# Adaptive max pooling over windows of 16: three stores to memory become two

## The chip, the cores and the metric

The kernel runs on one core of a Trainium2 chip. The metric is the device time of one execution in microseconds, the median of several runs. Three engines matter here: VectorE (DVE in the profile) reduces, SyncE (SP) issues the loads and most stores, ScalarE (ACT) issues one store. The transfers themselves are carried out by the core's 16 DMA engines, whoever issues them.

## The reference

The input is 32 x 256 x 4096 numbers of 4 bytes (134.2 MB), the output 32 x 256 x 256 (8.4 MB). Since 4096 divides evenly by 256, every output is the maximum over 16 neighbours.

```python
batch, channels, length = 32, 256, 4096
output_size = 256
...
for i in range(output_size):
    start = int(i * length / output_size)
    end = int((i + 1) * length / output_size)
    result[:, :, i] = np.max(x[:, :, start:end], axis=-1)
```

## The kernel before

**Columns.** Rows and windows of the input are seen as one long list of windows of W = 16 numbers, 2,097,152 of them. Dealt out over the 128 partitions of the on-chip memory they make `total` = 16384 windows a partition, each of which gives one output column. The list is cut into two groups, of 9340 and 7044 columns a partition, one after the other in memory (`group`, line 64). Within a group each partition owns one unbroken stretch of input and of output, so a load or store is 128 long rows, one for each partition, with the group's length as the distance between rows.

**Loads.** `group_a` is one load of 128 columns, eight of 1024, and one of 1020; `group_b` is six of 1024 and one of 900 (`last`). A load of 1024 columns is 128 rows of 65,536 B, 8 MB. All loads are issued by SP in one queue (lines 87 and 96). The first group is taken from its end towards its beginning, the second from its beginning on.

**The ring.** Loads land in `ring`, two slots of 1024 columns with a GAP of 152 columns for each. Every second time a slot is used, the load is placed 152 columns further (`moved`). A load's reduction is split in two, of 872 and 152 columns (lines 98 to 101), the part that the next load into the slot overwrites going first, so that the next load may be issued when the larger part is done. The gaps leave room in the ring.

**Reductions.** VectorE does all of them, `pooled` on line 56: 32 instructions. Results go to the tile `kept` (15484 columns), but those of the last load, for which there is no room in `kept`, go into a free stretch of the ring (`last_kept`, lines 103 to 105).

**Stores.** Three. ScalarE stores the last 900 columns from the ring (line 114), rows of 3,600 B; it waits for the last reduction. After a scheduling barrier without waits (line 115), SP stores `kept` in two transfers (line 117), one for each group: 9340 columns (rows of 37,360 B), for which it waits for nothing that SP has not waited for already, and 6144 columns (rows of 24,576 B), for which it waits for the last reduction but one. SP's instructions run in the order of the program: 17 loads, then these two stores. Each load waits for the reduction that frees its place.

Of the kernel before, what the change touches and what calls it, by code (L numbers as in the profile page):

```python
# [1 line left out]

# [4 lines left out]


@with_exitstack
def kernel(  # L10
    ctx: ExitStack,
    tc: tile.TileContext,
    x: bass.AP,
    output_size: bass.AP,
    out: bass.AP,
):

    nc = tc.nc
    P = nc.NUM_PARTITIONS
    fp32 = mybir.dt.float32

    B, C, L = x.shape
    O = int(output_size)  # L30
    assert L % O == 0, (L, O)
    W = L // O
    total = B * C * O // P
    assert B * C * O % P == 0

    CHUNK = 1024
    GAP = 152
    FIRST = 128
    LOADS_A, LOADS_B = 9, 6

    LESS = 4
    group_a = [FIRST] + [CHUNK] * (LOADS_A - 1) + [CHUNK - LESS]
    last = total - sum(group_a) - LOADS_B * CHUNK
    group_b = [CHUNK] * LOADS_B + [last]
    assert 0 < last and last * (W + 1) <= CHUNK * W

    pool = ctx.enter_context(tc.tile_pool(name="pool", bufs=1))
    ring = pool.tile([P, 2 * (CHUNK + GAP) * W], fp32, tag="ring", name="ring")
    kept = pool.tile([P, total - last], fp32, tag="kept", name="kept")

    xw = x.flatten_outer_dims().rearrange("r (o w) -> (r o) w", w=W)
    ow = out.flatten_outer_dims().rearrange("r o -> (r o)")

    def pooled(dst, at, n):

        nc.vector.reduce_max(  # L56
            out=dst,
            in_=ring[:, at * W : (at + n) * W].rearrange("p (n w) -> p n w", w=W),
            axis=mybir.AxisListType.X,
        )  # L60

    taken = 0

    def group(n):

        nonlocal taken
        span = slice(taken * P, (taken + n) * P)
        taken += n
        return (
            xw[span].rearrange("(p n) w -> p (n w)", p=P),  # L70
            ow[span].rearrange("(p n) -> p n", p=P),
        )

    stores = []
    n_loads = 0
    base = 0
    for g, loads in enumerate((group_a, group_b)):
        xg, og = group(sum(loads))
        a = sum(loads) if g == 0 else 0
        for n in loads:  # L80
            if g == 0:
                a -= n
            xn = xg[:, a * W : (a + n) * W]
            dst = kept[:, base + a : base + a + n] if n != last else None
            if n == FIRST:

                nc.sync.dma_start(  # L87
                    out=ring[:, CHUNK * W : (CHUNK + n) * W], in_=xn
                )
                pooled(dst, CHUNK, n)  # L90
            else:

                low = n_loads % 2 * (CHUNK + GAP)
                moved = n_loads // 2 % 2
                at = low + moved * GAP
                nc.sync.dma_start(out=ring[:, at * W : (at + n) * W], in_=xn)
                if n != last:
                    cut = CHUNK - GAP if moved else GAP
                    parts = [(0, cut), (cut, n)]
                    for u, v in parts if moved else parts[::-1]:  # L100
                        pooled(dst[:, u:v], at + u, v - u)
                else:
                    end = (at + CHUNK) * W
                    last_kept = ring[:, end - n : end]
                    pooled(last_kept, at, n)
                n_loads += 1
            if g:
                a += n
        full = a - last if g else sum(loads)
        stores.append((og[:, 0:full], kept[:, base : base + full]))  # L110
        base += full
    assert taken == total

    nc.scalar.dma_start(out=og[:, full : full + last], in_=last_kept)
    tc.no_sync_barrier()
    for dst, src in stores:
        nc.sync.dma_start(out=dst, in_=src)


# [1 line left out]
_INS = ['x', 'output_size']  # L121
_OUTS = [((32, 256, 256), 'float32')]

_NUMBERS = {'output_size': 256}


# [26 lines left out]
```

## Time and profile before

| | us |
|---|---|
| median of 3 runs | 334.95 (334.94 to 335.01) |
| span of the profiled execution | 333.08 |
| VectorE busy | 276.5 |
| distance between two loads' landings | 19.35 |
| the two reductions of one load (872 + 152 columns) | 17.28 |
| VectorE's wait for each load | 2.07 |

The profile is of one execution; its span leaves out what lies around the program, here 1.87 us. A DMA issue on SP or ScalarE takes about 0.4 us of that engine; the transfer then goes on by itself, and "us to landing" is counted from the issue to the arrival of the last of 16 completion marks, one from each DMA engine. The trace also holds a record of every packet of every transfer, with start, duration, size and queue; here one packet is one row of one partition.

### The profile page before, as it was taken

To read this page: it belongs to the slowest core of one execution; us is meant where nothing else is said; L and a number is where in the kernel's file an instruction comes from. 1 tells how busy PE (TensorE), PEld (TensorE's weight loads), DVE (VectorE), ACT (ScalarE), POOL (GpSimd) and SP (SyncE) were. 2 spreads that over 40 slices of the span, in tenths; PEclk is the share of its full clock that TensorE was granted. 3 is DMA by queue.
4 is the path that set the end of the run, shared out by engine and by line. 5 is a ranking of instruction groups with operands and counts; after the bars stand their busy time and mean duration, and the time that the engine had idled before them with its cause. 6 is when DMAs were issued, how large, how long until landed. Compare 5 with 4: busy or idle time off the path is not lost.

```text
span 333.1 us, 113 instructions
## 1 busy us (share of the span) xinstructions
DVE 276.5 (83%) x32; POOL 0.2 (0%) x4
## 2 busy tenths in 40 slices
DVE  2009979797997979799797979979797998979993
POOL 0000000000000000000000000000000000000000
DMA  9898989899898989899898989899898989899997
GB/s 378 378 504 378 504 378 504 378 449 433 378 504 378 504 378 504 378 441 441 384 494 377 504 378 504 378 456 425 386 496 378 504 378 504 378 458 443 393 395 330
DMA packets 2880, 142.61 MB, mean 428 GB/s; under 512 B 320, under 2 KB 320, under 8 KB 448
## 3 DMA queue, kind: packets, MB, share of 16 engines
q1 hardware_dynamic: 2736, 142.15, 98.8%
q10 hardware_dynamic: 144, 0.46, 0.3%
HBM read 134.22 MB, written 8.39 MB: 428 GB/s over the span
## 4 chain that ended last, share of the span: by engine, by line
DMA 57%; DVE 36%; DVEq 5%; issue 0%; SPq 0%
DMA ring<-in_x_dram 57%; DVE kept L56 36%; DVEq L148 5%; SPq L87 0%
## 5 line engine op out<-in xcount | busy, mean ns | idle before, releaser
L56 DVE TENSOR_REDUCE kept<-ring 128x152 f32<-128x2432 f32 (+3 forms) x31 | 261.4, 8473 | 51.5 <-DMA ring<-in_x_dram 51.5
L56 DVE TENSOR_REDUCE ring<-ring 128x900 f32<-128x14400 f32 x1 | 15.1, 15143 | 0.0
L134 POOL MEMSET const-bfloat16-1.0<- 128x1 bf16 x1 | 0.1, 103 | 0.0
L134 POOL MEMSET const-uint8-127<- 128x1 uint8 x1 | 0.1, 102 | 0.0
L134 POOL MEMSET const-float32-0.0<- 128x1 f32 x1 | 0.1, 100 | 0.2 <-issue 0.2
L134 POOL MEMSET const-float32-1.0<- 128x1 f32 x1 | 0.1, 99 | 0.0
## 6 DMA issues: line engine op xcount, KB each, us to landing
ring<-in_x_dram SPq DMA_DIRECT2D x1, 8160.0 KB, 23.9
ring<-in_x_dram SPq DMA_DIRECT2D x1, 7200.0 KB, 21.7
out_dram<-kept SPq DMA_DIRECT2D x1, 4670.0 KB, 32.4
out_dram<-kept SPq DMA_DIRECT2D x1, 3072.0 KB, 18.2
ring<-in_x_dram SPq DMA_DIRECT2D x1, 1024.0 KB, 4.7
out_dram<-ring ACTq DMA_DIRECT2D x1, 450.0 KB, 4.2
ring<-in_x_dram SPq DMA_DIRECT2D x14, 24.0
```

What stands on the lines that cost most here:

```text
L56: nc.vector.reduce_max(out=dst, in_=ring[:, at * W : (at + n) * W].rearrange("p (n w) -> p n w", w=W), axis=mybir.AxisListType.X,)
L134: nc = _bacc.Bacc("TRN2", target_bir_lowering=False, num_devices=1)
L148: with _tile.TileContext(nc) as tc:
```

## The change

The two groups are cut elsewhere. The first now takes all loads but the last two: 128 columns, thirteen loads of 1024, one of 1020, which makes 14460 columns; the second takes the last two, of 1024 and 900 columns, 1924 in all. `kept` holds the first group alone. The second group's results all go to the last 1924 x 4 B of the ring (`tail_kept`). ScalarE stores these 1924 columns in one transfer (rows of 7,696 B), and SP the first group in one transfer (rows of 57,840 B). In the program ScalarE's store stands ahead of the barrier, as before. The engines' own order of instructions stays: SP has 17 loads and then one store, which waits for the 29th of VectorE's 32 reductions (the second one of the 1020-column load); VectorE has the same 32 reductions, the shorter of 868 columns now for the fifteenth load, not the tenth; the wait for the free stretch of the ring moves from the last reduction to the last but two.

```diff
-    LOADS_A, LOADS_B = 9, 6
-    LESS = 4
-    group_a = [FIRST] + [CHUNK] * (LOADS_A - 1) + [CHUNK - LESS]
-    last = total - sum(group_a) - LOADS_B * CHUNK
-    group_b = [CHUNK] * LOADS_B + [last]
+    LAST = 900
+    n_head = (total - FIRST - CHUNK - LAST) // CHUNK
+    short = total - FIRST - CHUNK - LAST - n_head * CHUNK
+    head = [FIRST] + [CHUNK] * n_head + [short]
+    tail = [CHUNK, LAST]
+    n_a, n_b = sum(head), sum(tail)
...
-    kept = pool.tile([P, total - last], fp32, tag="kept", name="kept")
+    kept = pool.tile([P, n_a], fp32, tag="kept", name="kept")
...
+    xa = xw[: n_a * P].rearrange("(p n) w -> p (n w)", p=P)
+    oa = ow[: n_a * P].rearrange("(p n) -> p n", p=P)
+    xb = xw[n_a * P :].rearrange("(p n) w -> p (n w)", p=P)
+    ob = ow[n_a * P :].rearrange("(p n) -> p n", p=P)
...
+    work = []
+    a = n_a
+    for n in head:
+        a -= n
+        work.append((n, xa[:, a * W : (a + n) * W], kept[:, a : a + n]))
+    tail_kept = ring[:, size - n_b :]
+    a = 0
+    for n in tail:
+        work.append((n, xb[:, a * W : (a + n) * W], tail_kept[:, a : a + n]))
+        a += n
...
+    for i, (n, xn, dst) in enumerate(work[1:]):
+        moved = i // 2 % 2
+        at = i % 2 * (CHUNK + GAP) + moved * GAP
+        load(at, n, xn)
+        if i == len(work) - 2:
+            pooled(dst, at, n)
+            continue
+        cut = CHUNK - GAP if moved else GAP
+        parts = [(0, cut), (cut, n)]
+        for u, v in parts if moved else parts[::-1]:
+            pooled(dst[:, u:v], at + u, v - u)
...
-    nc.scalar.dma_start(out=og[:, full : full + last], in_=last_kept)
+    nc.scalar.dma_start(out=ob, in_=tail_kept)
     tc.no_sync_barrier()
-    for dst, src in stores:
-        nc.sync.dma_start(out=dst, in_=src)
+    nc.sync.dma_start(out=oa, in_=kept[:, :])
```

More of the change, by code (lines that the diff above doesn't have):

```diff
@@ L38 @@
     FIRST = 128
-    LOADS_A, LOADS_B = 9, 6
-    LESS = 4
-    group_a = [FIRST] + [CHUNK] * (LOADS_A - 1) + [CHUNK - LESS]
-    last = total - sum(group_a) - LOADS_B * CHUNK
-    group_b = [CHUNK] * LOADS_B + [last]
-    assert 0 < last and last * (W + 1) <= CHUNK * W
-    pool = ctx.enter_context(tc.tile_pool(name="pool", bufs=1))
-    ring = pool.tile([P, 2 * (CHUNK + GAP) * W], fp32, tag="ring", name="ring")
-    kept = pool.tile([P, total - last], fp32, tag="kept", name="kept")
+    LAST = 900
+    n_head = (total - FIRST - CHUNK - LAST) // CHUNK
+    short = total - FIRST - CHUNK - LAST - n_head * CHUNK
+    assert 0 < short <= CHUNK
+    head = [FIRST] + [CHUNK] * n_head + [short]
+    tail = [CHUNK, LAST]
+    n_a, n_b = sum(head), sum(tail)
+    assert n_a + n_b == total
     xw = x.flatten_outer_dims().rearrange("r (o w) -> (r o) w", w=W)
     ow = out.flatten_outer_dims().rearrange("r o -> (r o)")
+    xa = xw[: n_a * P].rearrange("(p n) w -> p (n w)", p=P)
+    oa = ow[: n_a * P].rearrange("(p n) -> p n", p=P)
+    xb = xw[n_a * P :].rearrange("(p n) w -> p (n w)", p=P)
+    ob = ow[n_a * P :].rearrange("(p n) -> p n", p=P)
+    pool = ctx.enter_context(tc.tile_pool(name="pool", bufs=1))
+    size = 2 * (CHUNK + GAP) * W
+    ring = pool.tile([P, size], fp32, tag="ring", name="ring")
+    kept = pool.tile([P, n_a], fp32, tag="kept", name="kept")
     def pooled(dst, at, n):
@@ L60, in pooled @@
         )
[L62 to L111, printed above, removed]
@@ L112, with load @@
-    assert taken == total
-    nc.scalar.dma_start(out=og[:, full : full + last], in_=last_kept)
+    def load(at, n, xn):
+        nc.sync.dma_start(out=ring[:, at * W : (at + n) * W], in_=xn)
+    work = []
[8 more added lines that the diff above has]
+        a += n
+    n, xn, dst = work[0]
@@ new lines @@
+    load(CHUNK, n, xn)
+    pooled(dst, CHUNK, n)
+    for i, (n, xn, dst) in enumerate(work[1:]):
[3 more added lines that the diff above has]
+        if i == len(work) - 2:
+            assert (at + n) * W + n_b <= size
+            pooled(dst, at, n)
[4 more added lines that the diff above has]
+            pooled(dst[:, u:v], at + u, v - u)
```

## The prediction

> **What bounds the kernel now.** I read the page first, then the order in time, the transfers with their landings, and transfers alone in short windows near the end.
>
> ```profile
> span 333.1 us, 113 instructions
> ...
> DVE 276.5 (83%) x32; POOL 0.2 (0%) x4
> ...
> q1 hardware_dynamic: 2736, 142.15, 98.8%
> q10 hardware_dynamic: 144, 0.46, 0.3%
> ```
>
> q1 is the queue that SP issues to, q10 ScalarE's. Together their packets keep the 16 DMA engines busy for 99.1% of the span; VectorE is busy for 83%. Bytes through the DMA engines are the bound, and an edit that moves the same bytes can only win what lies at the two ends. What matters here is the end, in the order of time:
>
> ```profile
> 291.37 21.90 SPq L117 DMA_DIRECT2D out_dram<-kept  x2
> 295.62 17.28 DVE L56 TENSOR_REDUCE kept<-ring 128x872 f32<-128x13952 f32 x2 [2.07 <-DMA ring<-in_x_dram]
> 312.82 15.14 DVE L56 TENSOR_REDUCE ring<-ring 128x900 f32<-128x14400 f32 x1
> 327.99 0.37 ACTq L114 DMA_DIRECT2D out_dram<-ring  x1
> ```
>
> The last reduction has no idle time before it: from the landing of the last load but one (295.60 in the chain of waits) VectorE runs without a break to 327.97, and ScalarE's store goes out at 327.99. The transfers show what the DMA engines do meanwhile:
>
> ```profile
> ring<-in_x_dram SPq DMA_DIRECT2D x1, 7200.0 KB, 21.7
> out_dram<-kept SPq DMA_DIRECT2D x1, 4670.0 KB, 32.4
> out_dram<-kept SPq DMA_DIRECT2D x1, 3072.0 KB, 18.2
> ...
> out_dram<-ring ACTq DMA_DIRECT2D x1, 450.0 KB, 4.2
> ```
>
> The last load is issued at 290.99 and lands at 312.7. The first store, issued at 291.37, lands at 323.8, and the second, issued at 312.9, at 331.1. These are one after the other: 11.1 us for 4670 KB, then 7.3 us for 3072 KB. So SP's queue works in the order of issue, and a store issued early simply waits behind the load. ScalarE's 450 KB are issued at 327.99. Transfers in 327.90 to 330.19:
>
> ```profile
> DMA packets 32, 0.79 MB, mean 343 GB/s; under 512 B 0, under 2 KB 0, under 8 KB 0
> ## 3 DMA queue, kind: packets, MB, share of 16 engines
> q1 hardware_dynamic: 32, 0.79, 80.1%
> ```
>
> and in 330.19 to 331.80:
>
> ```profile
> q10 hardware_dynamic: 144, 0.46, 71.9%
> q1 hardware_dynamic: 16, 0.00, 0.6%
> ```
>
> Not one packet of q10 starts until SP's store is through (the 16 tiny packets of q1 are its completion marks). In the single packet records q10's first row starts 6 ns after q1's completion mark on the same engine. So today ScalarE's rows stand ready and the DMA engines set the end; VectorE has some slack, at most 2.2 us (327.99 to the first q10 packet at 330.20).
>
> **The change, part by part.** *Loads.* The same 17 load sizes in another order: the 1020-column one moves from tenth to fifteenth. The bytes before the last two loads are equal, so those land when they did. The rows of a load now lie 14460 x 64 = 925,440 B apart in memory instead of 597,760 B (first group) and 450,816 B (second). In the packet records a 65,536 B row took 2.418 to 2.4215 us in both groups: 0.0035 us x 8 rows on an engine x 16 loads = 0.45 us if all went from the best to the worst, but the mean by loads differs by only 0.002 us (2.4195 in the first group, 2.4215 in the second), which over the six loads of the second group is 8 x 6 x 0.002 = 0.1 us. Bounds -0.1 to +0.15 us (all nine of the first group at the second's rate); I take 0, as no row shows which pitch it would resemble.
>
> *VectorE.* The same 32 reductions. The pair for load 15 of 16 (14.69 + 2.68 us) now writes to the free end of the ring, not to `kept`; the last reduction already does that and takes 15.14 us for 900 columns, 16.82 ns a column, against 14.69/872 = 16.84 for `kept`. Cost 0. Its semaphore wait for that region (a reduction of long ago) moves from the last reduction to this pair, some 0.02 us, as the idle steps marked issue in the chain. VectorE ends at 327.97 as before; if these 0.02 us are exposed, the store is late by that.
>
> *SP's stores.* Two (4670 and 3072 KB) become one of 128 x 14460 x 4 B = 7230 KB (7.40 MB). It waits for the second reduction of load 14 of 16, which ends at 276.28 + 17.28 = 293.56. Behind it on SP's queue stands nothing but the end of the program. Issued at 293.6, it is queued 18 us before the last load leaves the DMA engines; that load hides the later issue (291.37 before). Without this cover, issued only with the next reduction at 312.9 as today's second store is, the engines would idle from 312.3 to 313.9 (one issue-to-first-packet time, below), about 1.6 us. One store less saves SP's issue (0.4 us, hidden) and eight descriptors on each engine.
>
> *ScalarE's store.* From 900 to 1924 columns: rows of 7,696 B, 985,088 B. It still waits for the last reduction.
>
> *Sum over one DMA engine, from the end of the last load.* Each store has 8 rows on each engine. Packet records: 37,360 B took 1.384 us in the mean, 24,576 B 0.916, 3,600 B 0.144. Before: 8 x (1.384 + 0.916 + 0.144) = 19.55 us. After: 57,840 B is nearest to the last load's 57,600 B (2.131), plus 240 B at (1.382 - 0.913)/12,784 B = 0.037 ns a byte: 2.140. 7,696 B is nearest to the first load's 8,192 B (0.309), less 0.018: 0.291. 8 x (2.140 + 0.291) = 19.45, and 19.49 with the 0.003 us by which stores' means lie over the shortest packet. Gain 0.06 to 0.10 us, if no engine has a gap.
>
> *The gap.* This is the price that decides. On the 16 engines the last load's packets end at 311.84 to 312.29, so the large store ends 17.12 us later, at 328.96 to 329.41, instead of 330.2 to 330.6. The cover over ScalarE's store shrinks by 1.2 us. When can its first packet start? It is issued at 327.99. One row shows a queue starting with nothing ahead: the first load, issued at 0.73. Transfers in 0.73 to 1.74, and in 1.74 to 2.20:
>
> ```profile
> DMA packets 0, 0.00 MB, mean 0 GB/s; under 512 B 0, under 2 KB 0, under 8 KB 0
> ...
> q1 hardware_dynamic: 16, 0.13, 156.1%
> ```
>
> Sixteen first packets, 1.02 to 1.43 us after the issue. For ScalarE: 329.01 to 329.42, the very moment at which the large store ends. The last engine then ends at 329.42 + 8 x 0.291 = 331.75; before, the last packet ended at 331.71 and the last completion arrived 0.52 us later (332.23). After: 332.27, that is +0.04 us. The other bound is a start as cold as the first load's: 4.7 us to landing less 8 x 0.309 = 2.23 us besides its rows; 327.99 + 2.23 + 2.33 = 332.55, +0.32 us. And the extreme: q10's first packet at the 2.21 us that the trace allows, 330.20, with the 0.43 us by which engines differ: 330.63 + 2.33 + 0.52 = 333.48, +1.25 us. Below, all dense: 332.13, -0.10 us. I take +0.15, between dense and cold: the engines are running here, which speaks for dense, but the tie is to within hundredths, and any hitch shows.
>
> The page "DMA: Bandwidth & Descriptors" of the Trainium skill (section on the anatomy of one DMA, measured on GpSimd's path) gives about 2.0 us fixed plus bytes over 436 GB/s; by that the store would land at 332.25, +0.02 us, an estimate from that page. The same page (section on queues, rings and completion order) says that an engine alternates between queues packet by packet; the windows above show the contrary here, q10 waiting for all of q1, and were the rule followed the small rows would slip in between the large ones, with the same total of busy time and no other end.
>
> **Forecast.** The end moves by -0.1 to +0.35 us, middle +0.15. Profiled span 333.08 to 333.23; the median of the runs lies 1.87 us over the profiled span (334.95 against 333.08), which carries over: 335.10 us. About 0.2% (0.67 us) is what a measurement of this kernel can tell from no change.
>
> **Rivals.**
> 1. *Late start (slower).* ScalarE's store, no longer under SP's, is exposed. Place: the gap on each engine between the last large row and the first 7.7 KB row. Price: whatever the first packet needs over 1.0 us. It becomes a loss of more than 0.67 us when the last engine's first packet comes after 330.05, that is 2.06 us after the issue, against 1.43 us in the first load. Time: up to 336.2, most likely 335.9. For: 2.21 us is not excluded by the trace. Against: the only row of an idle queue. 9%.
> 2. *Dense and better (faster side, still no change).* No gap, and all loads at the first group's pace: -0.10 - 0.10: 334.75. For: first-group rows are a trace quicker. Against: one slow engine of 16 undoes it. 15%. To be faster by more than 0.67 us, DMA time would have to vanish, of which the rows show 0.1 us at each place: 3%.
> 3. *The large store isn't early.* If it waits for a later reduction than the program's wait says (the 29th of 32, the one that ends at 293.56), 1.6 us of idle DMA: 336.6. 1%.
> 4. *Longer rows or wider pitch are slower.* 57,840 B rows or the 925,440 B pitch slowing every packet by 0.1% would give 0.3 us: 335.4. For: nothing but the 0.002 us between groups. It stays with the forecast; slow enough to show, 1%.
>
> The forecast itself has 71%, its own range 334.9 to 335.5. The range for 8 in 10 reaches down to the dense case and up into the late start: 334.7 to 335.7. Faster 3%, same 86%, slower 11%.
>
> **What would show it.** Right: one store of 7230 KB issued at about 293.6 and landing near 329.9; VectorE's last reduction ending at 328.0; ScalarE's store, 962 KB, landing 4.2 to 4.6 us after its issue; DMA share full until 329. Late start: a window around 329.5 without any packet, and 5 us or more to landing. Rival 3: SP's store issued at 313. Rival 4: the landing of load 15 of 16 later than 295.6. The forecast is wrong if VectorE ends at another time than 328.0, or if the DMA engines idle anywhere before 329.

## The result, and the profile after

The changed kernel takes 335.65 us (median of 16 runs, 335.40 to 336.04) against 335.01 (16 runs, 334.78 to 335.29) measured beside it: 0.64 us more, a ratio of 1.0019 with a 95% interval of 1.0012 to 1.0026. Measured again, with the experiments, it was 335.95 against 334.96, a ratio of 1.0030 (1.0019 to 1.0041). So the change costs 0.2 to 0.3%, at the edge of what was called no change; the forecast of 335.10 had the sign and a quarter of the size (0.15 against 0.64). The first median lies above the forecast's own range (334.9 to 335.5) and just inside the wider one (334.7 to 335.7), the second above both.

The page of the changed kernel, first its span and queues, then its stores (KB, us from issue to landing):

```profile
span 334.1 us, 112 instructions
...
q1 hardware_dynamic: 2592, 141.62, 98.1%
q10 hardware_dynamic: 144, 0.99, 0.7%
...
out_dram<-kept SPq DMA_DIRECT2D x1, 7230.0 KB, 36.2
...
out_dram<-ring ACTq DMA_DIRECT2D x1, 962.0 KB, 4.7
```

The DMA engines are busy for 98.8% of a span that is 0.99 us longer (this profiled execution took 335.85 us, above its median). ScalarE's store takes 4.7 us to landing, not 4.2. The order in time from the large store on:

```profile
293.96 0.35 SPq L96 DMA_DIRECT2D out_dram<-kept  x1
296.14 32.34 DVE L56 TENSOR_REDUCE ring<-ring 128x872 f32<-128x13952 f32 x3 [2.21 <-DMA ring<-in_x_dram]
328.51 0.37 ACTq L94 DMA_DIRECT2D out_dram<-ring  x1
```

The large store goes out at 294.0, as forecast (293.6), and lands at 330.2 (329.9). But VectorE's last three reductions start at 296.14 where before they started at 295.62, and the store follows at 328.51, 0.52 us later than before. The chain of waits shows a part of that (start, us, what):

```profile
272.16 23.89 DMA ring<-in_x_dram
296.05 0.03 issue
296.07 0.02 DVEq L56
296.10 0.05 issue
296.14 17.28 DVE ring L56 x2
```

The load itself lands 0.45 us later (296.05 against 295.60). Most of that is there by the third load, whose reduction stands here before and after:

```profile
44.13 17.28 DVE L56 TENSOR_REDUCE kept<-ring 128x872 f32<-128x13952 f32 x2 [2.07 <-DMA ring<-in_x_dram]
```

```profile
44.56 17.28 DVE L56 TENSOR_REDUCE kept<-ring 128x872 f32<-128x13952 f32 x2 [2.35 <-DMA ring<-in_x_dram]
```

The second load's reduction starts 0.16 us late (24.94 against 24.78), the third's 0.43: in this execution 0.27 us went in the third load itself, whose rows took up to 2.71 us instead of 2.42. Then, before the last load but one is reduced, VectorE steps through the added semaphore wait, 0.09 us to the start of the reduction where it was 0.02: the wait for the ring's free stretch, moved here, costs 0.07 us.

Last, the packets of the final microseconds. In 329.4 to 330.0 and in 332.0 to 333.0:

```profile
DMA packets 38, 0.27 MB, mean 449 GB/s; under 512 B 3, under 2 KB 3, under 8 KB 38
...
q10 hardware_dynamic: 35, 0.27, 118.1%
```

```profile
DMA packets 3, 0.02 MB, mean 15 GB/s; under 512 B 1, under 2 KB 1, under 8 KB 3
...
q10 hardware_dynamic: 3, 0.02, 3.7%
```

A record names no engine, but a row starts where the row before it on its engine ended, so rows can be put together by engine. ScalarE's 7.7 KB rows follow SP's large ones closely: the large store ends at 329.11 to 329.68, and q10's first rows start at 329.39 to 329.69. Thirteen engines stand empty for a moment (0.16 us in the mean of all 16). Yet after 332.0 three packets are left. They are one engine's: two rows and a completion mark. In the packet records its first q10 row, started 6 ns after the large store's completion mark, took 1.047 us, not 0.29, and this one engine ends 0.8 us after the other fifteen.

### The profile page after: what moved, and what is told of

Read it like the earlier page. It is cut to its first block, busy times and chain, and to the rows that moved or that the text cites. A ratio compares the mean times of both kernels' runs of the same rounds, so it can differ in the third digit from the quotient of the medians.

```text
span 334.1 us, 112 instructions
## 1 busy us (share of the span) xinstructions
DVE 276.5 (83%) x32; POOL 0.2 (0%) x4
## 4 chain that ended last, share of the span: by engine, by line
DMA 57%; DVE 36%; DVEq 5%; issue 0%; SPq 0%
DMA ring<-in_x_dram 57%; DVE kept L56 31%; DVE ring L56 5%; DVEq L127 5%; SPq L63 0%; DVEq L56 0%
## 5 line engine op out<-in xcount | busy, mean ns | idle before, releaser
L56 DVE TENSOR_REDUCE kept<-ring 128x152 f32<-128x2432 f32 (+3 forms) x29 | 244.1, 8458 | 49.8 <-DMA ring<-in_x_dram 49.8
L56 DVE TENSOR_REDUCE ring<-ring 128x872 f32<-128x13952 f32 (+2 forms) x3 | 32.3, 10835 | 2.2 <-DMA ring<-in_x_dram 2.2
```

The source lines that it names most:

```text
L56: nc.vector.reduce_max(out=dst, in_=ring[:, at * W : (at + n) * W].rearrange("p (n w) -> p n w", w=W), axis=mybir.AxisListType.X,)
```

## The experiments

There were two theories. The *tail theory*: ScalarE's store has lost its cover and its first rows start slowly. The *load theory*: the loads, with rows now 925,440 B apart, are slower. Twelve experiments were run, two of them repeats. Differences are against the kernel before, measured beside them: 334.96 for the first four (26 executions), 334.99 for the second four (29), 335.00 for the last four (21). Intervals are at 95%.

**The changed kernel again.** No edit.

> The changed kernel once more, for a second profile on the chip that also runs the three others. Both theories: 0.5 to 0.8 us over before. Tail theory (the 962 KB store has lost its cover, its first rows start cold): in this profile too, some engine's first row of that store takes 0.5 us or more instead of 0.29, and issue to landing is 4.5 us or more; the last load lands within 0.1 us of before's 312.7. Load theory (rows 925,440 B apart slow the loads): the last load lands 0.3 us or more after before's, and the store's first rows need not be slow.

335.95 us, +0.99, more than either theory expected. The store lands after 4.5 us; six of q10's first rows took 0.48 to 0.84 us. The last load lands at 313.0, against 312.7, and its packets end at 312.51, 0.22 us after before's 312.29. So there are slow first rows, as the tail theory has it, and a late last load, as the load theory has it.

**Its loads, with before's end.**

```diff
-    kept = pool.tile([P, n_a], fp32, tag="kept", name="kept")
+    kept = pool.tile([P, n_a + CHUNK], fp32, tag="kept", name="kept")
...
-    tail_kept = ring[:, size - n_b :]
+    tail_kept = [kept[:, n_a:], ring[:, size - LAST :]]
...
-    nc.scalar.dma_start(out=ob, in_=tail_kept)
+    nc.scalar.dma_start(out=ob[:, CHUNK:], in_=tail_kept[1])
     tc.no_sync_barrier()
-    nc.sync.dma_start(out=oa, in_=kept[:, :])
+    nc.sync.dma_start(out=oa, in_=kept[:, :n_a])
+    nc.sync.dma_start(out=ob[:, :CHUNK], in_=kept[:, n_a:])
```

> The changed kernel's loads (groups of 14460 and 1924 columns) with before's end: the last load but one goes to kept and is stored by SP (1024 columns) behind the large store, ScalarE stores 900 columns. Tail theory: back to before, -0.1 to +0.15 us, ScalarE's store lands about 4.2 us after its issue. Load theory: +0.4 to +0.7 us, as the changed kernel.

335.26 us, +0.30, ratio 1.0009 (1.0001 to 1.0018): under what the load theory asked, over what the tail theory allowed. The issues of this kernel:

```profile
ring<-in_x_dram SPq DMA_DIRECT2D x1, 1024.0 KB, 5.1
out_dram<-kept SPq DMA_DIRECT2D x1, 512.0 KB, 18.1
out_dram<-ring ACTq DMA_DIRECT2D x1, 450.0 KB, 4.2
```

ScalarE's store is back at 4.2 us; the first load takes 5.1 us to land, where before it took 4.7.

**Before's loads, with the changed end.**

```diff
-    kept = pool.tile([P, total - last], fp32, tag="kept", name="kept")
...
+    n_b = CHUNK + last
+    tail_kept = ring[:, size - n_b :]
+    kept = pool.tile([P, total - last - CHUNK], fp32, tag="kept", name="kept")
...
-            dst = kept[:, base + a : base + a + n] if n != last else None
+            in_tail = g and a >= (LOADS_B - 1) * CHUNK
+            dst = tail_kept[:, :CHUNK] if in_tail else kept[:, base + a : base + a + n]
...
-                    pooled(last_kept, at, n)
+                    pooled(tail_kept[:, CHUNK:], at, n)
...
-        full = a - last if g else sum(loads)
+        full = a - n_b if g else sum(loads)
...
-    nc.scalar.dma_start(out=og[:, full : full + last], in_=last_kept)
+    nc.scalar.dma_start(out=og[:, full : full + n_b], in_=tail_kept)
```

> Before's loads (groups of 9340 and 7044 columns) with the changed kernel's end: ScalarE stores the last 1924 columns from the ring, SP 9340 and 5120 columns, and the two reductions of the last load but one wait for the ring. Tail theory: +0.4 to +0.7 us, store landing 4.5 us or more after issue. Load theory: -0.1 to +0.15 us.

335.75 us, +0.79, ratio 1.0023 (1.0013 to 1.0034). The end alone is the larger part. The two parts add up to 1.09 us; both together, the changed kernel, cost 0.99 beside them and 0.64 in the first measurement. Its issues and the end in time:

```profile
out_dram<-ring ACTq DMA_DIRECT2D x1, 962.0 KB, 5.1
```

```profile
295.79 32.34 DVE L59 TENSOR_REDUCE ring<-ring 128x872 f32<-128x13952 f32 x3 [2.16 <-DMA ring<-in_x_dram]
328.16 0.37 ACTq L117 DMA_DIRECT2D out_dram<-ring  x1
```

VectorE is only 0.17 us late (0.07 of it the moved wait); the store needs 5.1 us to land instead of 4.2. Thirteen of q10's first rows, one on each of 13 engines, took 0.41 to 1.40 us, eleven of them over 0.8, with almost no gap ahead of them: SP's 20 KB rows ran until the moment they started (6 ns after SP's completion mark on that engine for most).

**ScalarE's store in two, the first one early.**

```diff
-    nc.scalar.dma_start(out=ob, in_=tail_kept)
+    nc.scalar.dma_start(out=ob[:, :CHUNK], in_=tail_kept[:, :CHUNK])
+    nc.scalar.dma_start(out=ob[:, CHUNK:], in_=tail_kept[:, CHUNK:])
```

> The changed kernel with ScalarE's store in two: 1024 columns as soon as the last load but one is reduced (about 313.4), 900 columns at the end. Tail theory: ScalarE's first rows stand ready behind SP's store or go in between, none starts cold, and the end is back at before's, -0.1 to +0.15 us. Load theory: +0.4 to +0.7 us. Open in both: whether the early rows wait for all of SP's store or take turns with it.

335.23 us, +0.27, ratio 1.0009 (1.0000 to 1.0018), again between the two expectations: the time of the loads-only kernel. The tail's part is gone, and the rest stays. The open question has an answer, too. Transfers in 318 to 320, with the early store issued at 313.58:

```profile
q1 hardware_dynamic: 16, 0.93, 107.2%
q10 hardware_dynamic: 16, 0.07, 8.0%
```

One row of ScalarE's for each of SP's: the two queues take turns on every engine. But no row of q10 came before 318.3, 4.7 us after the issue, while two more 2.14 us rows of SP's went first; it seems that a row or two ahead were already given to each engine. These early first rows were not slow: each took 0.16 us, like those after them.

**The last store from SP.**

```diff
-    nc.scalar.dma_start(out=ob, in_=tail_kept)
     tc.no_sync_barrier()
     nc.sync.dma_start(out=oa, in_=kept[:, :])
+    nc.sync.dma_start(out=ob, in_=tail_kept)
```

> The changed kernel with its last store (1924 columns) issued by SP behind the large one, ScalarE issues nothing. If the slow first rows come from ScalarE's queue being idle before, they vanish on SP's busy queue: landing 4.2 us or less after issue, and the time is that of the loads-only kernel, +0.2 to +0.35 us over before. If they belong to any store issued less than some 2 us before the engines run empty, they stay: +0.6 to +1.0 us.

```profile
out_dram<-ring SPq DMA_DIRECT2D x1, 962.0 KB, 4.2
```

335.48 us, +0.49, ratio 1.0014 (1.0005 to 1.0022), between the two expectations. Its time alone decides nothing, but the trace does: the same bytes, nearly the same moment of issue (328.41), the same rows ahead, and no row took over 0.32 us. Slow first rows belong to ScalarE's queue when it starts from idle, not to a late store as such.

**ScalarE's queue used before.**

```diff
+    nc.scalar.dma_start(out=oa[:, :16], in_=kept[:, :16])
     nc.scalar.dma_start(out=ob, in_=tail_kept)
     tc.no_sync_barrier()
-    nc.sync.dma_start(out=oa, in_=kept[:, :])
+    nc.sync.dma_start(out=oa[:, 16:], in_=kept[:, 16:])
```

> The changed kernel with a small store of 16 columns taken from the large one and issued by ScalarE at about 294 us, so that its queue has run on all 16 engines before. If a queue's first use makes the first rows slow: they take 0.3 us here, and the time is +0.2 to +0.4 us over before. If the lost cover does: unchanged, +0.6 to +1.1 us, first rows up to 0.5 us or more on some engines.

```profile
out_dram<-ring ACTq DMA_DIRECT2D x1, 962.0 KB, 4.8
out_dram<-kept ACTq DMA_DIRECT2D x1, 8.0 KB, 21.3
```

335.89 us, +0.90, ratio 1.0029 (1.0018 to 1.0040). A store issued 34 us earlier, and landed 13 us earlier, warms nothing: first rows again took up to 1.13 us. That it was the queue's first use is ruled out.

**Half of the cover back.**

```diff
-    nc.scalar.dma_start(out=ob, in_=tail_kept)
+    nc.scalar.dma_start(out=ob[:, 512:], in_=tail_kept[:, 512:])
     tc.no_sync_barrier()
     nc.sync.dma_start(out=oa, in_=kept[:, :])
+    nc.sync.dma_start(out=ob[:, :512], in_=tail_kept[:, :512])
```

> The changed kernel with 512 of ScalarE's 1924 columns given back to SP, behind the large store: 8 rows of 2,048 B on each engine, about 0.7 us more cover, 1412 columns left for ScalarE. Tail theory: part of the loss comes back, +0.3 to +0.5 us, between the changed kernel (+0.64 to +0.99) and the loads-only one (+0.30). If cover does not matter: as the changed kernel.

```profile
out_dram<-ring ACTq DMA_DIRECT2D x1, 706.0 KB, 4.1
```

335.31 us, +0.32, ratio 1.0013 (1.0004 to 1.0021). With 0.7 us of SP's rows ahead of ScalarE's the median is that of the loads-only kernel, so the whole tail is back; its interval alone (+0.13 to +0.70) could not tell the whole from the half, but no slow row is left. From the packet records, with three kernels that are told of below (us; the two columns on when rows begin count from the issue of the last store):

| kernel | SP's last row ahead begins | first rows of the last store begin | longest row, usual row | landing |
|---|---|---|---|---|
| before | 1.3 to 1.7 | 2.2 to 2.6 | 0.16, 0.14 | 4.2 |
| its loads, before's end | 1.6 to 2.4 | 1.8 to 2.5 | 0.16, 0.15 | 4.2 |
| half cover | 1.1 to 1.7 | 1.2 to 1.8 | 0.25, 0.22 | 4.1 |
| cut at 12 | 1.7 to 2.0 | 2.2 to 2.5 | 0.16, 0.14 | 4.2 |
| cut at 5 | 0.6 to 1.0 | 2.1 to 2.5 | 0.15, 0.14 | 4.2 |
| cut at 2 | 0.1 to 0.6 | 2.1 to 2.6 | 0.53, 0.14 | 4.3 |
| before's loads, changed end | 0.1 to 0.5 | 0.9 to 1.3 | 1.40, 0.29 | 5.1 |
| changed | before the issue | 0.9 to 1.2 | 1.05, 0.29 | 4.7 |
| queue used before | before the issue | 0.9 to 1.2 | 1.13, 0.29 | 4.8 |
| last store from SP | before the issue | 0.8 to 1.0 | 0.32, 0.29 | 4.2 |

The kernel cut at 2 shows that time under cover is not what counts. Its last store waits 2.1 us or more behind SP's rows, as long as before's, and yet 14 of its 16 first rows took 0.24 to 0.53 us instead of 0.14:

```profile
out_dram<-ring ACTq DMA_DIRECT2D x1, 450.0 KB, 4.3
```

What sorts the table, its bottom line apart, is when SP's last row ahead begins. The slow rows of this kernel stand behind rows that began 0.09 to 0.50 us after the issue, its two usual ones behind rows that began at 0.57; cut at 5, with every last row at 0.59 or later, has no slow row, nor have the others above it. This order was read from the profiles afterwards, and no run was made to test it alone.

**The load part.** Some 0.3 us remain with a mended end. Three kernels cut the groups elsewhere: before with `LOADS_A, LOADS_B` of 2 and 13, 5 and 10, or 12 and 3 instead of 9 and 6. The kernel before ran once more, without an edit. The last is the loads-only kernel with the small first load drawn from the last group:

```diff
-    head = [FIRST] + [CHUNK] * n_head + [short]
-    tail = [CHUNK, LAST]
+    head = [CHUNK] * n_head + [short]
+    tail = [FIRST, CHUNK, LAST]
...
+    work.insert(0, work.pop(-3))
...
```

> Before with its groups cut after two loads: 2172 and 14212 columns, so that the first loads' rows lie 139,008 B apart instead of 597,760 B, and the later ones' 909,568 B. ScalarE's store is before's. If the cold start of the first loads costs more the farther their rows are apart (4.7 us to the first landing at 597,760 B, 4.8 to 5.3 us at 925,440 B): first landing 4.7 us or less, -0.4 to 0 us against before. If wide rows cost over all loads: +0.2 to +0.4 us, since 14 of 16 large loads are wide.

> The kernel before once more, for a second profile of its start. If the start of the loads depends on the groups: first landing 4.7 us or less, and the last load lands within 0.05 us of 312.7, as in the first profile. If the start merely varies from run to run: a first landing of 4.8 us or more is as likely as not.

> The loads-only kernel (+0.30 us), with the first small load taken from the last group: its 128 rows lie 131,328 B apart instead of 925,440 B, and the sixteen large loads stay wide (917,248 B). If the cold first rows cost more when they are far apart: first landing 4.7 us or less, 0 to +0.1 us over before. If the cost is in the large loads: +0.25 to +0.4 us.

> Before with its groups cut after twelve large loads: 12412 and 3972 columns, rows of the first loads 794,368 B apart. End as before. If distance costs, evenly: +0.15 to +0.25 us, between before (597,760 B) and the loads-only kernel (925,440 B, +0.30). If it is something else of the cut at fourteen: 0 to +0.1 us.

> Before with its groups cut after five large loads: 5244 and 11140 columns, rows of the first loads 335,616 B apart, of the later ones 712,960 B. End as before. If distance of the first rows costs: 0 to -0.3 us. If only the cut at fourteen costs: 0 to +0.1 us.

Two large loads in the first group: 335.13 us, +0.14, ratio 1.0004 (0.9995 to 1.0013), first landing 4.8 us; neither expectation. Five: 335.01, ratio 0.9999 (0.9990 to 1.0008), first landing 4.9. Twelve: 335.04, ratio 1.0001 (0.9992 to 1.0010), first landing 4.8. Before again: one run of 334.84, first landing 4.6. So a cost that grows evenly with the distance between rows is out: with the first loads' rows 336 KB, 598 KB and 794 KB apart the time is the same, and only the cut at fourteen (925 KB) is dearer. A cost that sets in above 794 KB is not ruled out. Nor is the changed program itself: all kernels cut at fourteen are edits of it, all others in this table are edits of before. From the packet records (us from the span's start):

| loads | second load ends | last load ends |
|---|---|---|
| before's groups, 3 profiles | 24.3 to 24.4 | 312.27 to 312.30 |
| cut at 2, 5 or 12, one each | 24.5 to 24.6 | 312.27 to 312.37 |
| cut at 14, 7 profiles | 24.5 to 25.0 | 312.38 to 312.69 |

The last loads of the seven end 0.23 us later in the mean than those of the six (312.53 against 312.30), though the ranges only just miss each other; the second load is already 0.27 us late (24.74 against 24.46). So in the mean it is the start, the first rows on each engine, and not the rate. It is not so in each profile: in the first one of the changed kernel more went in the third load, as shown above, and the cuts at 2, 5 and 12 start late, too, without a loss in time that is clear of the noise. One profile of each kernel is too few for more. Why this cut starts more slowly stays open.

The last kernel, with the small first load drawn from the last group, took 338.82 us, +3.8, ratio 1.0119 (1.0104 to 1.0134), as no theory had it. It changes several things at once: its last group has 2052 columns, so rows of the last two loads lie 131,328 B (128 KiB + 256 B) apart, and those of the stores 8,208 B (8 KiB + 16 B); and only fourteen, not sixteen, of the large loads stayed wide. Its issues:

```profile
ring<-in_x_dram SPq DMA_DIRECT2D x1, 7200.0 KB, 22.2
...
out_dram<-ring ACTq DMA_DIRECT2D x1, 450.0 KB, 7.0
```

The last load is 0.5 us slower, and ScalarE's 450 KB land 7.0 us after the issue, though the last packet ended at 333.32: 2.4 us until the completion arrives, where before has 0.52. Of its start alone something can be read: with compact first rows the first landing was 4.9 us, no faster.

No version beats the kernel before; cuts at 5 and 12 equal it.

## Why the prediction was off in size

*The bound and the order.* Right: the DMA engines are full to 329, VectorE's work is the same, the large store is issued at 294.0 and hidden behind the last load. Rivals 2 (dense and better) and 3 (the large store late) fell. But two of its own signs went against it: VectorE ended at 328.5, not 328.0, and ScalarE's store took 4.7 us to land, not 4.2 to 4.6. The first median lies in the wide range because the late start had been drawn into it, not because the sum of +0.15 was right.

*Loads.* Taken as 0 with bounds of -0.1 to +0.15; measured +0.23 us at the end of the last load and +0.30, +0.27 and +0.32 us in three kernels with this cut and a mended end. The bounds came from the steady rate of a row, which hardly changes (median 2.419 us before, 2.418 after); the start, for which only one cut was on view, was not in the sum. This term was missing. Rival 4 (longer rows or wider pitch) had the sign and the size: the landing of load 15 of 16 was to be later than 295.6, and came at 296.05, and 0.3 us is what it priced. Its place, a little on every packet, is not what the profiles show.

*VectorE.* The moved wait was put at 0.02 us; it costs 0.07, and it is exposed where engines now stand empty until ScalarE's rows come.

*The sum over one engine.* 19.45 to 19.49 us, and the rows took what was worked out (57,840 B in 2.139 us for 2.140, 7,696 B in 0.29 to 0.31 for 0.291).

*The gap.* Right in place and in time: q10's first packets were predicted at 1.02 to 1.43 us after the issue and came after 0.88 to 1.18, just as the large store ended. But the cost of starting was looked for ahead of the first packet, and it lies inside it: the first rows themselves take up to 1.4 us, and the engine with the slowest sets the end. This was on view before: the prediction took the start of the first load's rows from the trace, but those 8 KB rows, the first on each engine, themselves took 0.34 to 1.06 us instead of 0.31. Only the "cold" case had it in its 2.23 us besides the rows, priced at +0.32 us, and that case is what came: 2.37 us in the changed kernel's profile, 2.15 when it ran again, 2.49 with the queue used before, 2.72 with before's loads. In the first of these profiles the store lands 0.98 us later than before: 0.32 for cold, 0.14 above it, and 0.52 for the late issue. The end alone costs +0.79 us (interval +0.44 to +1.14 from the ratio). So rival 1 had about the right size, with another reason: the gap that it named stayed small, and its sign, a window around 329.5 without any packet, did not come. A late start deserved more than 9%.

*A reading that was wrong.* That q10 waits for all of q1 was concluded from a window with three rows of SP's left, which seems too few to see turns. The early store shows the two queues alternating row by row, after two more of SP's rows on each engine. The Trainium skill, page "DMA: Bandwidth & Descriptors", section on queues, rings and completion order, says that an engine goes round the queues packet by packet; the runs agree with it (16 rows each in 318 to 320), against the prediction.

## What to carry to other kernels

Where transfers are the bound, merging stores moves no bytes, so ask only what the last transfer hides behind: here 0.7 us of another queue's rows ahead of the final store was the difference between +0.32 us and +0.64 to +0.99 us. Leave a small piece to the end, behind rows of the busy queue that begin well after it is issued (0.6 us or more in these profiles). Issuing the last store on the queue that is busy also kept its rows from being slow, though its time (+0.49 us, interval +0.17 to +0.74) does not show how much that is worth. And cutting memory into other groups changes every row distance at once: measure the new cut by itself before crediting or blaming the edit that came with it. When a profile has a cold start anywhere, read how long its first rows took, and not only when they began.

## What was not expected of the hardware

The first rows of a store on a queue that starts from idle took 0.4 to 1.4 us instead of 0.29, on many engines without a gap ahead of them, when they started within 1.3 us of the issue. Rows that began 2.1 us or more after it were slow, too, in one kernel (0.24 to 0.53 us instead of 0.14), where the other queue's last row had begun at most 0.50 us after the issue. Where that row began 0.53 us or more after it, no first row was slow, and neither were the same rows on the busy queue. What inside the engine does this isn't shown.

The kernel with rows 8,208 B apart in its last stores, and loads 131,328 B apart just ahead, took 3.8 us longer in all, with 2.4 us between last packet and completion and rows of up to 0.50 us instead of 0.14 in ScalarE's store; whether one of the two does it, and which, wasn't separated. The Trainium skill, page "DMA: Bandwidth & Descriptors", section "Latency and other measured facts", reports copy rates that fall to half at row distances of 4 MiB against 512 KiB, and that +192 B on top of 4 MiB didn't help; no run here had such distances.
